# Hybrid decoder step on one core: all page loads of a round in one run, state loads in program order, the prompt tokens' attention norm on its own, one product on GpSimd

## The chip, the cores and the metric

The kernel runs on one core of a Trainium2 chip. The metric is the time of one execution on the device in microseconds (us). Work is issued by five queues: PE (TensorE: matmuls and, shown apart as PEld, their weight loads), DVE (VectorE), ACT (ScalarE), POOL (GpSimd) and SP (SyncE, which here issues nearly all DMA transfers). Each engine runs its own instructions in a fixed order; semaphores tie them together.

## The reference

One layer of a hybrid decoder for 256 prompt tokens and 8 samples of 8 new tokens each, 320 tokens (`NT`) in all, of width 2048. Everything is in float32.

```python
h = rmsnorm(x);  q, k, v, z, xbc, dt, glu = split(h @ w_in)
att = rmsnorm_per_head(stick_breaking_attention(q, k_all, v_all))
      # samples: 1024 past positions each, in pages of 128 from a pool, plus their own tokens
y   = rmsnorm(ssd(silu(conv(xbc)), dt, state) * silu(z))
u   = silu(layernorm(conv31(glu_u * sigmoid(glu_gate))))
x   = x + concat(att, y, u) @ w_out
x   = x + (silu(conv3(gate)) * val) @ w_down      # gate, val = split(rmsnorm(x) @ w_up)
return rmsnorm(x), new keys and values, all new states
```

Stick-breaking attention gives past position j the weight sigmoid(z_j) times the product of (1 - sigmoid(z_m)) over all m between j and the query. So it is computed from the newest page back to the oldest, with a running product as carry. The page table says which page of the pool holds which positions, so the address of a page load is known only at run time.

## The kernel before

**Weights.** Activations lie with channels on partitions and the 320 tokens in the free dimension. Every product with a weight matrix is built from *granules* of 128 x 1024 weights (512 KB). `wgran` loads one into a buffer `raw` (3 of them), ScalarE rounds it into `hi` (3), VectorE subtracts for the rest `lo` (3). `part` then does three matmuls for each of the eight 128x128 pieces: `hi` with the high and the low part of the activations and `lo` with the high part, 24 matmuls of 320 columns. A *block* is one 128-channel output of a projection: two granules of w_in, 48 matmuls into one `mm` tile. `win(b)` is block b of w_in. The sequence is: q, k, v and glu blocks, then `win(12)` to `win(23)` for xBC (each followed by a convolution in `g_xbc`, tiles `pre`, `xac`, `sgx`, `xs`), then z, then w_out, w_up and w_down. What the text calls block 20 is `win(20)`, in the instructions `mm_3829`; block 21 is `win(21)`, `mm_4070` before and `mm_4098` after.

**Work between the matmuls.** `part` calls `tick` after every fourth piece (12 matmuls). `tick` advances each generator of a list by one step (to its next `yield`), and so the small work is woven between the matmuls. A scheduler then orders the instructions of each engine. Inside `tc.high_priority()` an instruction is placed as early as its priority and its operands allow; weight loads and splits are written that way.

**The sample sweep.** `g_att` starts two `worker` generators. Each handles two pairs of samples, four *units* for each pair, from the newest quarter of the pages to the oldest; a unit is two samples times two pages. For a unit, `pages` reads four page numbers into registers of SP (from the second unit on through a copy `pu`, made on VectorE behind the previous unit's `m`), and `load` issues four DMAs of 256 KB into a `kt` or a `vt` tile. There are two buffers (`KVB`) for each of the tags `kt` and `vt`, shared by the two workers. So one *round* of both workers has 16 pages. A unit's steps: score matmuls (`mx<-kt,qpad`, 16), two sigmoids on ScalarE (`m` and `w`), a scan on VectorE (`cum`), the product of `w` and `cum` (line 566), two transposes (line 573), a copy to SBUF (line 577), 32 value matmuls (`av<-vt,m`), then the next unit's scores. When both workers have finished a group of samples, `g_pofin` transposes the result into `att`. The prompt's attention (`g_prompts`) ends earlier and writes `att[:, c, 64:]`.

**The attention norm.** `g_attnorm` starts when the whole sweep is done: squares on ScalarE, four matmuls with `blk2` that sum over a head's channels, a reciprocal root by Newton steps on VectorE (`rsq`, line 184, 12 instructions on the given number of columns), four matmuls with `blkT` that spread it over the channels, and a product with `att`.

**Behind w_out.** w_out is done in three passes over its 16 output blocks; the third (`mixY[1]`, granules of 128x512) also adds into `x2` and prepares `h2h`/`h2l`, the activations for w_up. `fst` is the FFN convolution's state, one load of 128x688. `g_state` runs in the w_up phase and updates 16 tiles `h0` of the SSD state.

Of the kernel before, what the change touches and what calls it, by code (L numbers as in the profile page):

```python
# [9 lines left out]
F32 = mybir.dt.float32  # L10
# [33 lines left out]
def body(ctx, tc, a):  # L44
# [469 lines left out]
    def pages(pr, hf, after=None):  # L514
        pu = pt[0:1].rearrange("p (s g) -> p s g", s=8)[:, 2 * pr:2 * pr + 2, 2 * hf:2 * hf + 2]
        if after is not None:
            q = ap.tile([1, 2, 2], I32, tag="pu", name=nm("pu"), bufs=2)
            V.scalar_tensor_tensor(out=q, in0=after[0:1, 0:4].bitcast(I32).rearrange("p (s g) -> p s g", s=2), scalar=0, in1=pu,
                                   op0=ALU.bitwise_and, op1=ALU.bitwise_or)
            pu = q  # L520
        with tc.high_priority():
            return [D.value_load(pu[0:1, e, j:j + 1], min_val=0, max_val=POOL - 1) for e in range(2) for j in range(2)]

    def load(tag, src, regs):
        t = ap.tile([P, 4, 512], F32, tag=tag, name=nm(tag), bufs=KVB)
        with tc.high_priority():
            for j, r in enumerate(regs):
                D.dma_start(out=t[:, j], in_=src[bass.ds(r, 1)].rearrange("a p n -> (a p) n"))
        return t


    def worker(prs):
        units = [(pr, hf) for pr in prs for hf in (3, 2, 1, 0)]
        regs = pages(*units[0])
        kt = load("kt", a["ck"], regs)
        vt = load("vt", a["cv"], regs)
        def scores(pr, kt):
            z = pmix()[:, 0:256]
            for e in range(2):
                for c in range(4):  # L540
                    mm(z[32 * c:32 * c + 32, :], qpad[:, c, 2 * pr + e], kt[:, 2 * e:2 * e + 2, c * P:(c + 1) * P], start=(e == 0), stop=(e == 1))
            return z

        yield
        z = scores(units[0][0], kt)
        for n, (pr, hf) in enumerate(units):
            gr = pr // 2
            if gr not in pos:
                pos[gr] = pav()
            po = [pos[gr][:, (2 * (pr % 2) + e) * P:(2 * (pr % 2) + e + 1) * P] for e in range(2)]  # L550
            yield
            m = keep(z, 256, nrow)
            w = take(z, 256, arow)
            if n + 1 < len(units):
                regs = pages(*units[n + 1], m)
                kt = load("kt", a["ck"], regs)
            for _ in range(2):
                yield
            while "self" not in done:
                yield  # L560
            if hf == 3:
                carry = cpair[:, pr:pr + 1]
            cum = ap.tile([P, 386], F32, tag="cum", name=nm("cum"), bufs=2)
            later(cum[:, 0:256], m, 256, carry)
            V.tensor_copy(cum[:, 256:257], carry)
            tt(V, w, w, cum[:, 1:257], ALU.mult)
            carry = car[:, pr:pr + 1]
            V.tensor_copy(carry, cum[:, 0:1])
            for _ in range(3):
                yield  # L570
            tp = pmix()[:, 0:256]
            for j in range(2):
                T.transpose(tp[:, j * P:(j + 1) * P], w[:, j * P:(j + 1) * P], ident)
            for _ in range(3):
                yield
            wT = t384("m")[:, 0:256]
            S.copy(wT, tp)
            for _ in range(2):
                yield
            if hf == 3:  # L580
                while len(gv) < 4 or any(g in gens for g in gv) or g_s[0] in gens:
                    yield
                for e in range(2):
                    for c in range(4):
                        mm(po[e][32 * c:32 * c + 32, :], wTm[:, 2 * pr + e, 32 * c:32 * c + 32], vtok[:, 0, c * P:(c + 1) * P],
                           start=(e == 0 and pr % 2 == 0))
            for e in range(2):
                for j in range(2):
                    for c in range(4):
                        mm(po[e][32 * c:32 * c + 32, :], wT[:, j * P + 32 * c:j * P + 32 * c + 32], vt[:, 2 * e + j, c * P:(c + 1) * P],  # L590
                           stop=(hf == 0 and j == 1))
            if n + 1 < len(units):
                z = scores(units[n + 1][0], kt)
                vt = load("vt", a["cv"], regs)
            if hf == 0:
                nseq[gr] += 1
                if nseq[gr] == 2:
                    gf.append(spawn(g_pofin(gr)))
# [72 lines left out]
        done.append("prompts")  # L671

    def g_attnorm():
        while gcv in gens:
            yield
        asq = rot.tile([P, 40, 38], F32, tag="uh", name="asq", bufs=1).rearrange("p a b -> p (a b)")[:, 0:4 * NT].rearrange("p (c t) -> p c t", c=4)
        act(asq, att, AF.Square)
        for _ in range(2):
            yield
        ps = pmix()  # L680
        for c in range(4):
            mm(ps[32 * c:32 * c + 32, :NT], blk2, asq[:, c], start=True, stop=True)
        ra = rsq(ps[:, 0:NT], NT, 64, "a", t320)
        for _ in range(3):
            yield
        for c in range(4):
            pb = pmix()
            mm(pb[:, :NT], blkT[:, c * P:(c + 1) * P], ra, start=True, stop=True)
            yield
            stt(V, att[:, c], att[:, c], col("gatt", c), pb[:, :NT], ALU.mult, ALU.mult)  # L690

    def g_att():
        g_s.append(spawn(g_self()))
        gp = spawn(g_prompts())
        wk = [spawn(worker([0, 2]))]
        for _ in range(5):
            yield
        wk.append(spawn(worker([1, 3])))
        while gp in gens or any(w in gens for w in wk) or any(g in gens for g in gf):
            yield  # L700
        done.append("att")
        yield from g_attnorm()
# [499 lines left out]
    h2h = [fp.tile([P, 8, NT], F32R, name=f"h2h{i}") for i in range(2)]  # L1202
    h2l = [t10("h2la", F32R), t10("h2lb", F32R)]
    acc2 = t320("acc2")
    for oc in range(KC):
        g0 = wgran(a["w_out"][oc, 1][:, 512:1024], 4)
        ps = pmain()
        mains(ps, [(g0, mixY[1][:, 0:4], mixY[1][:, 4:8])])
        xo = c2(x2, oc)
        with tc.high_priority():  # L1210
            tt(V, xo, xo, ps, ALU.add)
            act(c2(h2h, oc), xo, AF.Copy, scale=col("gffn", oc))
            stt(V, c2(h2l, oc), xo, col("gffn", oc), f32(c2(h2h, oc)), ALU.mult, ALU.subtract)
        sq = t320("sq")
        act(sq, xo, AF.Square)
        if oc == 0:
            G.tensor_copy(acc2, sq)
        else:
            tt(V if oc == KC - 1 else G, acc2, sq, acc2, ALU.add)
    rbs = []  # L1220


    fst = fp.tile([P, FC, 8, 2], F32, name="fst")
    D.dma_start(out=fst, in_=a["fst"])
    fso = fp.tile([P, FC, 18], F32, name="fso")
    gpre = [fp.tile([P, 338], F32, name=f"gpre{i}") for i in range(3)]
    for pr in gpre:
# [49 lines left out]
    def g_state():  # L1277
        for g in range(2):
            for k in range(2):
                ss = [2 * k, 4 + 2 * k, 2 * k + 1, 5 + 2 * k]  # L1280
                bm = fp.tile([P, P], F32, tag="bm", name=nm("bm"), bufs=2)
                hs = []
                for i, s in enumerate(ss):
                    r = slice(32 * i, 32 * i + 32)
                    ts(G, bm[r], bS[r, g], smask2[r, s:s + 1], ALU.mult)
                    h0 = fp.tile([P, 512], F32, tag="h0", name=nm("h0"), bufs=6)
                    D.dma_start(out=h0, in_=a["h0"][g, s])
                    tt(G, h0.rearrange("p (h d) -> p h d", h=8), h0.rearrange("p (h d) -> p h d", h=8),
                       ets[:, 16 * s + 8 * g:16 * s + 8 * g + 8].unsqueeze(2).to_broadcast([P, 8, 64]), ALU.mult)
                    hs.append(h0)  # L1290
                    for _ in range(3):
                        yield
                pss = [pmix() for _ in ss]
                for i in range(4):
                    r = slice(32 * i, 32 * i + 32)
                    mm(pss[i], bm[r], xS[g][r], start=True, stop=True)
                yield
                for i, s in enumerate(ss):
                    tt(V, hs[i], hs[i], pss[i], ALU.add)
                    D.dma_start(out=a["o_ss"][g, s], in_=hs[i])  # L1300
                    for _ in range(2):
                        yield
# [148 lines left out]
```

## Time and profile before

| what | value |
|---|---|
| time, median of 3 runs | 1464.94 us (1461.44 to 1466.72) |
| the profiled execution's own time | 1461.63 us |
| its span in the profile | 1459.8 us |
| TensorE busy | 1429.8 us, 98% of the span |
| VectorE busy | 902.6 us, 62% |
| ScalarE busy | 619.4 us, 42% |
| GpSimd busy | 192.4 us, 13% |
| data moved by DMA | 254.51 MB, 174 GB/s over the span |

The span runs from the first to the last instruction of the profiled execution; its own time is that span and what lies around it. Busy shares are means over stages: the sweep over the pages is one of them, and lies between about 80 and 280 us. What bounds a stage is read from the waits of the engine that is busiest there.

### The profile page before, as it was taken

To read this page: it belongs to the slowest core of one execution; us is meant where nothing else is said; L and a number is where in the kernel's file an instruction comes from. 1 tells how busy PE (TensorE), PEld (TensorE's weight loads), DVE (VectorE), ACT (ScalarE), POOL (GpSimd) and SP (SyncE) were. 2 spreads that over 40 slices of the span, in tenths; PEclk is the share of its full clock that TensorE was granted. 3 is DMA by queue.
4 is the path that set the end of the run, shared out by engine and by line. 5 is a ranking of instruction groups with operands and counts; after the bars stand their busy time and mean duration, and the time that the engine had idled before them with its cause. 6 is when DMAs were issued, how large, how long until landed. Compare 5 with 4: busy or idle time off the path is not lost.

```text
span 1459.8 us, 26793 instructions
## 1 busy us (share of the span) xinstructions
PE 1429.8 (98%) x10432; PEld 1386.5 (95%) x10432; DVE 902.6 (62%) x1636; ACT 619.4 (42%) x957; POOL 192.4 (13%) x321
## 2 busy tenths in 40 slices
PE   9999999899999999999999999999999999999996
PEld 8999998898889999999999999999999999999996
DVE  5577999868657885656545555455554555555455
ACT  6253555445544463334333443334433443433253
POOL 5000001112430431131100100001000110100000
PEclk9999999999999999999999999999999999999998
DMA  7566778774553554665544444544444444445442
GB/s 272 191 202 213 245 247 285 252 237 143 183 168 105 183 182 128 221 192 188 174 154 150 145 157 147 148 156 145 151 153 146 154 149 147 154 148 162 153 146 100
DMA packets 90880, 254.51 MB, mean 174 GB/s; under 512 B 10754, under 2 KB 17154, under 8 KB 90754
## 3 DMA queue, kind: packets, MB, share of 16 engines
q1 hardware_dynamic: 90754, 252.80, 54.6%
q8 instruction: 82, 1.34, 0.4%
q14 instruction: 44, 0.36, 0.1%
HBM read 242.67 MB, written 9.77 MB: 173 GB/s over the span
## 4 chain that ended last, share of the span: by engine, by line
PE 86%; DVE 8%; issue 2%; DMA 2%; ACT 1%; SPq 0%; DVEq 0%; ACTq 0%
PE mm L69 79%; PE mx L69 4%; DVE cfc L78 2%; DVE lo L72 2%; PE av L69 2%; DVE xac L78 1%; DMA kt<-in_ck 1%; DVE cum L479 0%; ACT hi L87 0%; DMA x0a<-in_x 0%; DMA raw<-in_w_out 0%; DVE w L72 0%; DVE x2a L72 0%; PE mx L962 0%; ACT uh L781 0%
## 5 line engine op out<-in xcount | busy, mean ns | idle before, releaser
L87 ACT ACTIVATE hi<-raw 128x1024 fp32r<-128x1024 f32 (+2 forms) x396 | 396.8, 1002 | 650.4 <-PE mm L69 401.2
L72 DVE TENSOR_TENSOR lo<-raw,hi 128x1024 fp32r<-128x1024 f32 (+2 forms) x396 | 467.3, 1180 | 266.7 <-ACT hi L87 265.6
L69 PE MATMUL mm<-h2h,hi 128*128 128x320 f32 x1376 | 425.9, 309 | 0.1
L69 PE MATMUL mm<-h2h,lo 128*128 128x320 f32 x1376 | 423.3, 308 | 0.0
L69 PEld LDWEIGHTS mm<-h2h,hi 128*128 128x128 f32 x1376 | 258.3, 188 | 3.4 <-issue 1.9
L69 PEld LDWEIGHTS mm<-h2h,lo 128*128 128x128 f32 x1376 | 258.3, 188 | 0.8 <-DVE lo L72 0.8
L69 PE MATMUL mm<-abh,hi 128*128 128x320 f32 x688 | 212.9, 309 | 0.4 <-DVE x2a L72 0.2
L69 PE MATMUL mm<-abh,lo 128*128 128x320 f32 x688 | 212.6, 309 | 0.0
L69 PE MATMUL mm<-h2la,hi 128*128 128x320 f32 x688 | 212.6, 309 | 0.0
L69 PE MATMUL mm<-h2lb,hi 128*128 128x320 f32 x688 | 212.6, 309 | 0.0
L69 PE MATMUL mm<-abl,hi 128*128 128x320 f32 x688 | 212.5, 309 | 0.0
L69 PEld LDWEIGHTS mm<-abh,hi 128*128 128x128 f32 x688 | 129.1, 188 | 1.2 <-issue 1.1
L69 PEld LDWEIGHTS mm<-abl,hi 128*128 128x128 f32 x688 | 129.2, 188 | 0.0
L69 PEld LDWEIGHTS mm<-h2lb,hi 128*128 128x128 f32 x688 | 129.1, 188 | 0.0
L69 PEld LDWEIGHTS mm<-abh,lo 128*128 128x128 f32 x688 | 129.1, 188 | 0.0
L69 PEld LDWEIGHTS mm<-h2la,hi 128*128 128x128 f32 x688 | 129.1, 188 | 0.0
L69 PE MATMUL mm<-xhb,hi 128*128 128x320 f32 x288 | 92.3, 321 | 0.0
L69 PE MATMUL mm<-xha,hi 128*128 128x320 f32 x288 | 90.9, 316 | 0.0
L69 PE MATMUL mm<-xla,hi 128*128 128x320 f32 x288 | 89.6, 311 | 1.3 <-DVE xla L78 1.3
L69 PE MATMUL mm<-xlb,hi 128*128 128x320 f32 x288 | 90.0, 312 | 0.0
L69 PE MATMUL mm<-xhb,lo 128*128 128x320 f32 x288 | 89.8, 312 | 0.0
L69 PE MATMUL mm<-xha,lo 128*128 128x320 f32 x288 | 89.1, 309 | 0.0
(355 smaller groups left out, 1932.1 us busy)
## 6 DMA issues: line engine op xcount, KB each, us to landing
raw<-in_w_up SPq DMA_DIRECT2D x172, 512.0 KB, 3.6
raw<-in_w_in SPq DMA_DIRECT2D x80, 512.0 KB, 3.7
raw<-in_w_dn SPq DMA_DIRECT2D x80, 512.0 KB, 3.5
kt<-in_ck SPq DMA_DIRECT2D x64, 256.0 KB, 3.9
vt<-in_cv SPq DMA_DIRECT2D x64, 256.0 KB, 4.6
h<-in_h SPq DMA_DIRECT2D x32, 256.0 KB, 4.3
raw<-in_w_out SPq DMA_DIRECT2D x16, 512.0 KB, 3.7
raw<-in_w_out SPq DMA_DIRECT2D x32, 256.0 KB, 2.7
```

The source lines that it names most:

```text
L69: T.matmul(out, lhsT, rhs, start=start, stop=stop, skip_group_check=True)
L72: e.tensor_tensor(out=out, in0=x, in1=y, op=op)
L78: e.scalar_tensor_tensor(out=out, in0=x, scalar=s, in1=y, op0=op0, op1=op1)
L87: S.activation(out, x, f, bias=bias, scale=scale)
```

## The change

1. `pages` and `load` put their work at a priority far above all other (`offset=10 ** 7`), so also above the weights.
2. The product of `w` and `cum` in the sample sweep (line 566) goes from VectorE (`V`) to GpSimd (`G`).
3. `g_attnorm` now handles the 64 sample columns only. A new generator `g_attnorm_p` handles the 256 prompt columns: it starts 24 ticks after the prompt's attention is done, during the sample sweep, and the sweep's end waits for it.
4. `fst` is loaded in the third pass of w_out, at output block 6, and `fst` and the `h0` loads of `g_state` are kept in program order (`keep_in_program_order`) rather than placed early by the scheduler.

```diff
--- before.py
+++ after.py
@@ -518,12 +518,12 @@
             V.scalar_tensor_tensor(out=q, in0=after[0:1, 0:4].bitcast(I32).rearrange("p (s g) -> p s g", s=2), scalar=0, in1=pu,
                                    op0=ALU.bitwise_and, op1=ALU.bitwise_or)
             pu = q
-        with tc.high_priority():
+        with tc.high_priority(offset=10 ** 7):
             return [D.value_load(pu[0:1, e, j:j + 1], min_val=0, max_val=POOL - 1) for e in range(2) for j in range(2)]
 
     def load(tag, src, regs):
         t = ap.tile([P, 4, 512], F32, tag=tag, name=nm(tag), bufs=KVB)
-        with tc.high_priority():
+        with tc.high_priority(offset=10 ** 7):
             for j, r in enumerate(regs):
                 D.dma_start(out=t[:, j], in_=src[bass.ds(r, 1)].rearrange("a p n -> (a p) n"))
         return t
@@ -563,7 +563,7 @@
             cum = ap.tile([P, 386], F32, tag="cum", name=nm("cum"), bufs=2)
             later(cum[:, 0:256], m, 256, carry)
             V.tensor_copy(cum[:, 256:257], carry)
-            tt(V, w, w, cum[:, 1:257], ALU.mult)
+            tt(G, w, w, cum[:, 1:257], ALU.mult)
             carry = car[:, pr:pr + 1]
             V.tensor_copy(carry, cum[:, 0:1])
             for _ in range(3):
@@ -671,32 +671,60 @@
         done.append("prompts")
 
     def g_attnorm():
-        while gcv in gens:
-            yield
-        asq = rot.tile([P, 40, 38], F32, tag="uh", name="asq", bufs=1).rearrange("p a b -> p (a b)")[:, 0:4 * NT].rearrange("p (c t) -> p c t", c=4)
-        act(asq, att, AF.Square)
+        b = slice(0, NS)
+        asq = t320("asq")[:, 0:256].rearrange("p (c t) -> p c t", c=4)
+        act(asq, att[:, :, b], AF.Square)
         for _ in range(2):
             yield
         ps = pmix()
         for c in range(4):
-            mm(ps[32 * c:32 * c + 32, :NT], blk2, asq[:, c], start=True, stop=True)
-        ra = rsq(ps[:, 0:NT], NT, 64, "a", t320)
+            mm(ps[32 * c:32 * c + 32, :NS], blk2, asq[:, c], start=True, stop=True)
+        ra = rsq(ps[:, 0:NS], NS, 64, "a")
+        for _ in range(2):
+            yield
+        pb = pmix()
+        for c in range(4):
+            mm(pb[:, NS * c:NS * c + NS], blkT[:, c * P:(c + 1) * P], ra, start=(c == 0), stop=True)
+        yield
+        for c in range(4):
+            stt(V, att[:, c, b], att[:, c, b], col("gatt", c), pb[:, NS * c:NS * c + NS], ALU.mult, ALU.mult)
+
+
+    def g_attnorm_p():
+        while "prompts" not in done:
+            yield
+        for _ in range(24):
+            yield
+        b = slice(NS, NT)
+        sq = [t384("m")[:, 0:256] for _ in range(4)]
+        for c in range(4):
+            act(sq[c], att[:, c, b], AF.Square)
         for _ in range(3):
+            yield
+        ps = pmix()
+        for c in range(4):
+            mm(ps[32 * c:32 * c + 32, :256], blk2, sq[c], start=True, stop=True)
+        ra = rsq(ps[:, 0:256], 256, 64, "a", lambda s: t320(s)[:, 0:256])
+        for _ in range(6):
             yield
         for c in range(4):
             pb = pmix()
-            mm(pb[:, :NT], blkT[:, c * P:(c + 1) * P], ra, start=True, stop=True)
-            yield
-            stt(V, att[:, c], att[:, c], col("gatt", c), pb[:, :NT], ALU.mult, ALU.mult)
+            mm(pb[:, :256], blkT[:, c * P:(c + 1) * P], ra, start=True, stop=True)
+            yield
+            stt(V, att[:, c, b], att[:, c, b], col("gatt", c), pb[:, :256], ALU.mult, ALU.mult)
+        done.append("attp")
 
     def g_att():
         g_s.append(spawn(g_self()))
         gp = spawn(g_prompts())
+        spawn(g_attnorm_p())
         wk = [spawn(worker([0, 2]))]
         for _ in range(5):
             yield
         wk.append(spawn(worker([1, 3])))
         while gp in gens or any(w in gens for w in wk) or any(g in gens for g in gf):
+            yield
+        while "attp" not in done:
             yield
         done.append("att")
         yield from g_attnorm()
@@ -1202,7 +1230,10 @@
     h2h = [fp.tile([P, 8, NT], F32R, name=f"h2h{i}") for i in range(2)]
     h2l = [t10("h2la", F32R), t10("h2lb", F32R)]
     acc2 = t320("acc2")
+    fst = fp.tile([P, FC, 8, 2], F32, name="fst")
     for oc in range(KC):
+        if oc == 6:
+            tc.keep_in_program_order(D.dma_start(out=fst, in_=a["fst"]))
         g0 = wgran(a["w_out"][oc, 1][:, 512:1024], 4)
         ps = pmain()
         mains(ps, [(g0, mixY[1][:, 0:4], mixY[1][:, 4:8])])
@@ -1220,8 +1251,6 @@
     rbs = []
 
 
-    fst = fp.tile([P, FC, 8, 2], F32, name="fst")
-    D.dma_start(out=fst, in_=a["fst"])
     fso = fp.tile([P, FC, 18], F32, name="fso")
     gpre = [fp.tile([P, 338], F32, name=f"gpre{i}") for i in range(3)]
     for pr in gpre:
@@ -1284,7 +1313,7 @@
                     r = slice(32 * i, 32 * i + 32)
                     ts(G, bm[r], bS[r, g], smask2[r, s:s + 1], ALU.mult)
                     h0 = fp.tile([P, 512], F32, tag="h0", name=nm("h0"), bufs=6)
-                    D.dma_start(out=h0, in_=a["h0"][g, s])
+                    tc.keep_in_program_order(D.dma_start(out=h0, in_=a["h0"][g, s]))
                     tt(G, h0.rearrange("p (h d) -> p h d", h=8), h0.rearrange("p (h d) -> p h d", h=8),
                        ets[:, 16 * s + 8 * g:16 * s + 8 * g + 8].unsqueeze(2).to_broadcast([P, 8, 64]), ALU.mult)
                     hs.append(h0)
```

`t384("m")`, `t320` and `pmix` are the existing rotating tiles of the attention part; `stt`, `tt` and `act` are the kernel's short names for operations of VectorE or GpSimd and of ScalarE, as the lines above show.

The orders below are lists of instructions as they stand in one engine's program. First SP (DMA issues) around the w_in granule `raw_2568`, the second one of `win(12)`. `TENSOR_LOAD pu` is the reading of a page number, `ISA` a register instruction. Before:

```order
L528 DMA kt_2299<-in_ck 128x512
L124 DMA raw_2568<-in_w_in 128x1024
L522 ISA x2
L522 TENSOR_LOAD pu_2308
L522 ISA x2
L522 TENSOR_LOAD pu_2261
L528 ISA
L528 DMA kt_2299<-in_ck 128x512
L124 DMA raw_2807<-in_w_in 128x1024
```

After, at the same granule:

```order
L528 ISA
L528 DMA kt_2346<-in_ck 128x512
L522 ISA x4
L124 DMA raw_2568<-in_w_in 128x1024
L124 DMA raw_2807<-in_w_in 128x1024
L124 DMA raw_2813<-in_w_in 128x1024
```

Pages and granules took turns before; now the last of 16 pages (`vt_2201`, `vt_2231`, `kt_2299`, `kt_2346`, four each) stands ahead of `raw_2568`, and granules follow each other.

Next TensorE inside block 20 (`mm_3829`), before. `vt_3493` and `vt_3531` are value pages of the last round but two, `kt_3608` and `kt_3655` key pages of the last round but one:

```order
L69 MATMUL mm_3829<-xhb,lo_3824 128x320
L69 MATMUL av_3066<-vt_3493,m_3842 32x128 x16
L69 MATMUL mx_3900<-kt_3608,qpad 32x256 x8
L69 MATMUL av_3066<-vt_3531,m_3844 32x128 x16
L69 MATMUL mx_3930<-kt_3655,qpad 32x256 x8
L69 MATMUL mm_3829<-xhb,hi_3825 128x320
```

After, behind the last matmul of the same block 20 (`mx_3967` are the sums of the prompt norm, `mx_4240` to `mx_4313` its products with `blkT`; `vt_3917`, `vt_3947` belong to the last round but one, the tiles from `kt_4029` on to the last):

```order
L69 MATMUL mm_3829<-xhb,lo_3824 128x320
L69 MATMUL mx_3967<-m_3842,blk_200 32x256
L69 MATMUL mx_3967<-m_3843,blk_200 32x256
L69 MATMUL mx_3967<-m_3844,blk_200 32x256
L69 MATMUL mx_3967<-m_3845,blk_200 32x256
L573 MATMUL mx_4210<-ident,w_3989 128x128 x2
L573 MATMUL mx_4213<-ident,w_4036 128x128 x2
L69 MATMUL av_3066<-vt_3917,m_4277 32x128 x16
L69 MATMUL av_3066<-vt_3947,m_4279 32x128 x16
L69 MATMUL mx_4240<-r_3973,blkT 128x256
```

And directly on, up to the first matmuls of block 21:

```order
L69 MATMUL mx_4313<-r_3973,blkT 128x256
L69 MATMUL mx_4356<-kt_4029,qpad 32x256 x8
L69 MATMUL mx_4386<-kt_4076,qpad 32x256 x8
L573 MATMUL mx_4534<-ident,w_4416 128x128 x2
L69 MATMUL av_3066<-vt_4365,m_4596 32x128
L573 MATMUL mx_4537<-ident,w_4420 128x128 x2
L69 MATMUL av_3066<-vt_4365,m_4596 32x128 x15
L69 MATMUL av_3066<-vt_4395,m_4598 32x128 x16
L609 MATMUL mx_4688<-ident,m_4689 128x128 x2
L609 MATMUL mx_4688<-ident,m_4706 128x128 x2
L69 MATMUL mm_4098<-xha,hi_4088 128x320
L69 MATMUL mm_4098<-xla,hi_4088 128x320
```

Before, each step of the sweep stood between matmuls of w_in, and the last rounds were spread over the matmuls of six more blocks (to the 69th granule of w_in). Now the last two rounds stand in one piece behind block 20 (the 57th and 58th granule), without a w_in matmul between them.

Last SP near the end of w_out, before:

```order
L1224 DMA fst<-in_fst 128x688
L124 DMA raw_6563<-in_w_out 128x512
L1287 DMA h_7283<-in_h 128x512
L124 DMA raw_6588<-in_w_out 128x512
L1287 DMA h_7323<-in_h 128x512
L1287 DMA h_7389<-in_h 128x512
L124 DMA raw_6613<-in_w_out 128x512
```

After:

```order
L124 DMA raw_6701<-in_w_out 128x512
L1236 DMA fst<-in_fst 128x688
L124 DMA raw_6727<-in_w_out 128x512
L124 DMA raw_6752<-in_w_out 128x512
L124 DMA raw_6777<-in_w_out 128x512
```

`fst` stands five granules of w_out later, and the `h0` tiles (`h` here) no longer stand between them.

## Rows read from the trace of the kernel before

**Rows 1.** Page: the span; busy time, share and instructions of each engine.

```profile
span 1459.8 us, 26793 instructions
PE 1429.8 (98%) x10432; PEld 1386.5 (95%) x10432; DVE 902.6 (62%) x1636; ACT 619.4 (42%) x957; POOL 192.4 (13%) x321
```

**Rows 2.** Waits of PE: waiting instruction, awaited one: us in total, times, longest.

```profile
PE mx L69 <- DMA kt<-in_ck: 7.0, 4, 2.3
PE mx L69 <- DVE r L78: 5.4, 3, 2.4
PE mm L69 <- DVE x2a L72: 2.4, 3, 1.5
PE mx L573 <- DVE w L72: 1.8, 1, 1.8
```

**Rows 3.** Timeline of PE: start, duration, instruction, [idle before <-releaser].

```profile
271.57 1.08 PE L69 MATMUL av<-vt,m 128*32 128x128 f32 x32
272.47 1.05 PE L69 MATMUL mx<-kt,qpad 128*32 128x256 f32 x16
...
278.77 0.81 PE L69 MATMUL mx<-kt,qpad 128*32 128x256 f32 x8 [1.98 <-DMA kt<-in_ck]
...
356.65 1.31 PE L69 MATMUL mx<-r,blkT 128*128 128x320 f32 x4 [1.16 <-DVE r L78]
```

**Rows 4.** Windows: busy of PE, PEld, DVE, ACT, POOL; clock, DMA share, GB/s.

```profile
144.00:148.00 4.00, 4.00 (x31) 3.64 (x30) 1.37 (x4) 2.17 (x4) 0.00 (x0) 1.00 1.04 388
200.00:250.00 50.00, 47.75 (x481) 45.27 (x483) 48.49 (x118) 27.94 (x61) 8.18 (x10) 1.00 0.84 274
279.20:282.60 3.40, 3.40 (x16) 3.09 (x13) 1.35 (x5) 0.84 (x2) 0.00 (x0) 0.51 1.02 357
```

**Rows 5.** Waits of the SP queue.

```profile
SPq L124 <- DVE lo L72: 975.5, 368, 5.8
```

**Rows 6.** Timeline of SP: DMA issues in the sweep.

```profile
139.48 5.11 SPq L528 DMA_DIRECT2D vt<-in_cv  x8
...
260.27 0.34 SPq L124 DMA_DIRECT2D raw<-in_w_in  x1
262.00 0.33 SPq L528 DMA_DIRECT2D kt<-in_ck  x1
```

**Rows 7.** Page, DMA issues: transfer, count, KB each, median us to landing.

```profile
raw<-in_w_in SPq DMA_DIRECT2D x80, 512.0 KB, 3.7
kt<-in_ck SPq DMA_DIRECT2D x64, 256.0 KB, 3.9
```

**Rows 8.** Chain in order of time: start, us, work.

```profile
118.42 7.04 PE mm L69 x48
```

**Rows 9.** Groups by shape, 60:345 (DVE 60:370): count | busy, mean ns | idle.

```profile
L87 ACT ACTIVATE hi<-raw 128x1024 fp32r<-128x1024 f32 x61 | 64.7, 1060 | 96.9 <-PE mm L69 57.4 <-issue 30.2 <-PE mx L69 3.1
L87 ACT ACTIVATE m<-mx,nrow 128x256 f32<-128x256 f32 x16 | 7.5, 470 | 15.6 <-PE mx L69 14.5 <-ACT w L87 0.9
...
L577 ACT COPY m<-mx 128x256 f32<-128x256 f32 x16 | 5.5, 370 | 2.0 <-PE mx L573 2.0
...
L72 DVE TENSOR_TENSOR lo<-raw,hi 128x1024 fp32r<-128x1024 f32 x65 | 80.9, 1244 | 25.0 <-ACT hi L87 24.8
...
L479 DVE TENSOR_TENSOR_SCAN cum<-m,car,zero 128x256 f32<-128x256 f32 x12 | 9.2, 763 | 2.8 <-ACT m L87 2.8
...
L72 DVE TENSOR_TENSOR q<-r 128x320 f32<-128x320 f32 x3 | 1.5, 485 | 0.0
```

**Rows 10.** Page, costliest groups, of GpSimd: count | busy, mean ns | idle.

```profile
L72 POOL TENSOR_TENSOR fac<-fac,rb 128x320 f32<-128x320 f32 x43 | 37.7, 876 | 41.8 <-ACT fac L87 41.8
```

**Rows 11.** Timeline of POOL and DVE at 273 to 277 us.

```profile
274.11 1.73 POOL L72 TENSOR_TENSOR xs<-xac,sgx 128x320 f32<-128x320 f32 x1 [0.71 <-ACT sgx L87]
...
273.45 0.55 DVE L78 SCALAR_TENSOR_TENSOR cfc<-uh,cols,cfc 128x320 f32<-128x320 f32 x1
...
275.05 1.14 DVE L78 SCALAR_TENSOR_TENSOR cfc<-uh,cols,cfc 128x320 f32<-128x320 f32 x1
```

## The prediction

> **What bounds the kernel now.** I read the page first [rows 1]: the profiled execution spans 1459.8 us (1461.63 us as timed, 1.8 us around it) and TensorE is busy in 98% of it. So there is little to win: whatever does not shorten a wait of TensorE or take matmul work away is hidden. Then the waits of TensorE [rows 2]: 7.0 us in four waits for key pages, 5.4 us in three waits for a reciprocal root (2.4 us of them at the kernel's end, which the change leaves alone), 2.4 us behind the add into `x2a`, 1.8 us before one transpose of `w`. Then the matmuls at those places [rows 3]: the score matmuls start after 1.98 us of idle time for `kt`, the normalising ones after 1.16 us for `r`. Last the windows [rows 4]: where two idle pieces stood close together, the granted clock falls to its lower level (1.2 GHz, 0.51 in the window) for 3.4 us, behind the key pages at 279 us and once more, in the same way, behind the attention norm at 361 us. At half rate 3.4 us do 1.7 us of work, so each costs 1.7 us more.
>
> Why the pages are late is on the SP queue. A weight load waits until its raw buffer is free, that is for a `lo` split [rows 5]; 368 of these waits add up to 975.5 us, and pages stand behind them in the same queue. In [rows 6] a weight load goes at 260.27 and the page behind it only at 262.00. The data path itself is not full over a whole sweep: DMA is busy 0.84 at 200 to 250 us, against 1.04 at 388 GB/s in a burst [rows 4].
>
> **The change, part by part.**
>
> *Pages in one run.* The two high priorities put all 16 pages of a round (8 of `vt`, 8 of `kt`, 256 KB each) ahead of the weights, as the first pair of orders shows. A round of 16 pages is 4.2 MB, 10.8 us at 388 GB/s; the issue alone runs at 5.1 us for 8 [rows 6], 10.2 us for 16. A page lands 3.9 us after its issue [rows 7]. A round of the sweep has about five weight granules of 3.5 us each (48 matmuls in 7.04 us [rows 8]) between one use and the next, so the pages land well before their score matmuls. I take all four waits as gone: -7.0 us, and with them the low clock behind them, -1.7 us.
>
> What stands behind the run are the weights, and TensorE waits for those. Three raw and three split buffers let SP issue a granule when TensorE has finished the sixth one before it and the split (1.06 + 1.24 us, [rows 9]) is done: 5 x 3.5 - 2.3 = 15.2 us ahead, plus the round's attention work on TensorE (two value products at 1.08, two scores at 1.05, [rows 3], some transposes at 0.15 each: 4.9 us) = 20.1 us. Needed: 10.8 us for the burst, 1.4 us for the 512 KB at the same rate, 2.3 us of landing beyond that (3.7 less 1.4, [rows 7]), 2.3 us of split = 16.8 us. It fits by 3.3 us, so I take 0; the bound above is a rival below.
>
> *One product on GpSimd.* The 256-column product has no row on GpSimd. Between a 128x320 product of 0.88 us [rows 10] and one of 1.73 us [rows 11] I take 1.2 us, as the latter is the nearer in place. In the sweep three ticks lie between product and transpose, so most of it is covered by matmuls. The one wait of 1.8 us came from the product standing behind a split and a convolution step on VectorE, and on GpSimd nothing stands ahead of it: -1.6 us (from 0 to -1.8).
>
> A multiply of GpSimd costs VectorE something too: beside the one at 274.11 a convolution step takes 1.14 us instead of 0.55 [rows 11]. The Trainium skill says more, in "SBUF — State Buffer" (the section on the shared port pair): a VectorE instruction with two SBUF inputs and a GpSimd instruction that reads SBUF take turns on an exclusive lock. By the row each of the 16 products costs VectorE 0.6 us and spares it 0.4 (the price of 256 columns below); by the rule it would cost up to the whole 1.2 us, 19 us in all against 6 spared, in a stretch where VectorE has 1.5 idle us in 50 [rows 4]. Either way VectorE pays first with convolution steps that nobody waits for, so the sum takes 0 and the rule becomes a rival.
>
> *Prompt norm in the sweep.* Work on TensorE is unchanged: the same four sums and four products, split into 256 and 64 columns. What is left at the old place is a chain over 64 columns instead of 320. The waits there are 5.4 - 2.4 = 3.0 us; VectorE's split loads still stand inside the chain and the next norm's chain follows, so I take half, -1.5 us (0 to -3.0), and the low clock at 361 us as avoided, -1.7 us.
>
> *The knot behind block 20.* This is the price, and it is seen only in the order. `vt_4365` and `vt_4395`, the last value pages, wait for buffers that the round before frees, and the weights of block 21 stand behind them in SP's queue. So TensorE's order has no weights there: behind block 20 come the norm's sums, the transposes and value products of the last round but one, the norm's four products, the scores of the last round, its transposes, its value products, the final transposes, and only then block 21. Before, six blocks' matmuls lay between these steps. Counted from the end of block 20:
> - The root's chain is 12 VectorE instructions of 256 columns; at 0.485 us for 320 columns [rows 9] that is about 0.39 each, 4.7 us, and six steps of the block's own convolution lie in between, at the same price 2.3 us: `r` at 7.6 us with the sums (four matmuls at the pace of 48 in 7.04 us, 0.6). The transposes and value products of the round before (2.8 us) hide in it. The last pages of `kt` wait for the same round's page numbers and land at about the same time.
> - Four normalising products: two of 320 columns took 1.31 us [rows 3], so 2.1 us. Two scores 2.1 us: 11.8.
> - Then a bare chain for the second worker [rows 9]: sigmoid 0.47, scan 0.76, product on GpSimd 1.2, transpose 0.3, copy 0.37, value product 1.1, two copies 0.74, the `hi` split behind them in ScalarE's order 1.06, the `lo` split 1.24, 7.2 us together, and 0.8 that I put for some ten handovers: 8.0 us, so block 21 runs from 19.8 us.
> Matmuls in it: 0.6 + 2.8 + 2.1 + 2.1 + 0.6 + 2.2 + 0.6 = 11.0 us, so TensorE idles 8.8 us. The idle pieces lie as closely as those before the two falls of the clock, so I add two low stretches, one inside and one under block 21: 2 x 1.7 = 3.4. Sum +12.2 us. Bounds: 6 (clock stays up, root at 5 us) and 18 (three low stretches, a slow product, pages 3 us late).
>
> *State loads held in place.* Before, `fst` and six `h0` loads were pulled between the last w_out granules, and the wait behind `x2a` (2.4 us) is there. Now `fst` comes alone before a later granule and the `h0` loads come in w_up, where raw buffers are far ahead. -2.2 us (0 to -2.4).
>
> Sum: -7.0 - 1.7 - 1.6 - 1.5 - 1.7 - 2.2 + 12.2 = -3.5, so 1458.1 us against the profiled execution's 1461.63. The median of the three runs is 3.3 us above that execution; I put the forecast on the median, 1464.94 - 3.5 = **1461.4 us**. A measurement of this kernel can tell about 0.3% (4.4 us) from no change, so this counts as the same.
>
> **The rivals.**
> 1. *A cheap knot.* The clock stays up and the root comes early: +6 in place of +12.2, with all else as above: 1464.94 - 9.7 = 1455.2. For it: the longest wait for `kt` [rows 2], in the same sweep at 226 us and alone, brought no fall. Against: the knot has four of them in a row.
> 2. *Weights starve behind the pages* (slower). If SP must wait inside the run, for a page number or a freed buffer, by more than the 3.3 us of room, TensorE waits for a weight in each of six rounds. With 5.0 us inside, 1.7 us over the room, that is six times 1.7 and one low stretch: +12, 1473. For it: DMA is at 1.04 in bursts and at 0.84 over the sweep. Against: the buffers and numbers are freed within one short group of matmuls.
> 3. *A long knot.* Late pages or a third low stretch: +18, so 1467.2. It counts as the same.
> 4. *The lock.* GpSimd's products stop VectorE long enough to delay splits at 200 to 250 us, where it is busy 48.49 of 50 us: 16 x 0.8 us (1.2 held up less 0.4 spared), half of it on splits that are waited for: +6.4, 1467.8. Against: the row's 0.6 us would leave 0.2 of the 0.8. The rule of the Trainium skill above ("SBUF — State Buffer") is the one by which it would happen.
>
> **How the numbers follow.** The sum has 0.45, the cheap knot 0.25, starving 0.15, the long knot 0.1, the lock 0.05. The sum's own range is 1456 to 1467 (knot 8 to 18). For the whole, 1454 to 1470 leaves out most of the starving case and the best of the cheap one. Faster by over 0.3%: the cheap knot and a sixth of the sum's case, 0.32. Slower: starving, and a part of the long knot and the lock, 0.2. The same: 0.48.
>
> **What would show it.** Right: no wait for `kt` in 80 to 265 us; TensorE 15 to 25 us without w_in matmuls at about 270 to 292 us, with the granted clock at half there; no wait for `x2a` near 500 us. Wrong: waits for `hi` or `lo` right behind the page runs (rival 2), a knot whose idle time is under 5 or over 14 us, or VectorE's splits late beside GpSimd's products.

## The result, and the profile after

The changed kernel takes 1474.34 us (median of 4 runs, 1473.91 to 1475.97) against 1463.19 us of the kernel before (4 runs). The ratio is 1.0076, with a 95% interval of 1.0051 to 1.0102: slower by 11 us, where the prediction had 1461.4 us and no measurable change, with 0.2 on slower. The page of the changed kernel, its span and busy times:

```profile
span 1473.0 us, 26854 instructions
PE 1441.0 (98%) x10448; PEld 1394.5 (95%) x10448; DVE 902.0 (61%) x1636; ACT 620.5 (42%) x961; POOL 208.9 (14%) x337
```

The span is 13.2 us longer than in [rows 1], and TensorE's busy time rose by 11.2 us although its work is almost the same: part of that work ran at the lower clock. Now the waits of TensorE in the changed kernel:

```profile
PE mx L69 <- DVE r L78: 7.3, 3, 3.6
PE mm L69 <- ACT hi L87: 3.9, 4, 1.8
PE mm L69 <- DVE lo L72: 3.4, 3, 1.8
PE mx L69 <- ACT m L654: 1.2, 1, 1.2
PE mx L573 <- POOL w L72: 1.2, 1, 1.2
```

Against [rows 2], the waits for `kt` and `x2a` are gone, as forecast. New are 7.3 us of waits for weights (`hi` and `lo`), a wait of 3.6 us for the prompt norm's root, and 1.2 us for the product, now on GpSimd. Where the clock fell, in windows of the changed kernel (columns as in [rows 4]):

```profile
217.00:228.00 11.00, 8.00 (x86) 6.23 (x88) 8.77 (x17) 7.06 (x14) 1.80 (x3) 0.69 0.39 102
247.00:256.00 9.00, 6.94 (x65) 5.89 (x54) 7.93 (x13) 3.31 (x4) 1.49 (x2) 0.81 0.47 134
...
287.00:317.00 30.00, 22.03 (x210) 16.74 (x209) 16.08 (x47) 8.79 (x18) 3.43 (x5) 0.72 0.78 261
292.30:299.00 6.70, 5.81 (x28) 3.52 (x32) 2.63 (x6) 0.59 (x2) 0.86 (x1) 0.50 0.95 287
302.60:305.80 3.20, 3.20 (x58) 2.65 (x60) 0.00 (x0) 0.37 (x1) 0.00 (x0) 0.50 0.49 201
309.40:316.00 6.60, 6.06 (x23) 6.06 (x24) 4.34 (x11) 0.49 (x1) 0.00 (x0) 0.50 0.98 332
```

A granted clock of 0.69 over 11 us is (1 - 0.69) x 11 / 0.5 = 6.8 us at the lower level (1.2 GHz); the second row gives 3.4 us, the third 16.8 us. The kernel before had two such stretches of 3.4 us outside its end.

Two places hold the loss. First, **the weights behind the page runs**. SP, ScalarE, VectorE and TensorE of the changed kernel around the granule that follows the run at 194 us:

```profile
194.12 4.96 SPq L528 DMA_DIRECT2D vt<-in_cv  x8
199.60 8.43 SPq L528 DMA_DIRECT2D kt<-in_ck  x8
208.68 15.71 SPq L124 DMA_DIRECT2D raw<-in_w_in  x5
...
214.51 0.20 ACT L903 COPY sso<-pre 128x3 f32<-128x3 f32 x1 [3.53 <-DVE pre L72]
...
217.47 0.47 ACT L87 ACTIVATE sgx<-xac 128x320 f32<-128x320 f32 x1 [1.54 <-DVE xac L78]
217.84 1.04 ACT L87 ACTIVATE hi<-raw 128x1024 fp32r<-128x1024 f32 x1
...
217.35 2.79 DVE L78 SCALAR_TENSOR_TENSOR cfc<-uh,cols,cfc 128x320 f32<-128x320 f32 x4
220.06 1.22 DVE L72 TENSOR_TENSOR lo<-raw,hi 128x1024 fp32r<-128x1024 f32 x1
...
218.94 0.41 PE L69 MATMUL mm<-xha,hi 128*128 128x320 f32 x1 [1.16 <-ACT hi L87]
...
221.33 0.63 PE L69 MATMUL mm<-xha,lo 128*128 128x320 f32 x1 [1.84 <-DVE lo L72]
```

The run takes from 194.12 to 208.03, 13.9 us, not the 10.2 us that the prediction took for 16 issues: `kt x8` alone takes 8.43 us. Between these issues SP reads eight page numbers, some 0.27 us each, with register instructions behind them; for a number or a buffer that was not ready it waited only 0.4 us in this run. Then the granule issued at 208.68 is split only at 217.84 and 220.06. Transfers in this stretch landed after a median of 4.6 us:

```profile
raw<-in_w_in SPq DMA_DIRECT2D x3, 512.0 KB, 4.6
```

The rest of the delay is the order on the other engines: `hi` stands behind `sgx`, which waits for a convolution on VectorE, and `lo` behind four convolution steps. By that median the granule had landed at 213.3 us, while ScalarE stood idle up to 214.51 for the step ahead in its order. In the kernel before, the next split stood ahead of that step (line 903 is line 875 there):

```profile
211.08 1.06 ACT L87 ACTIVATE hi<-raw 128x1024 fp32r<-128x1024 f32 x1 [1.31 <-issue]
...
214.47 0.19 ACT L875 COPY sso<-pre 128x3 f32<-128x3 f32 x1 [2.07 <-DVE pre L72]
```

From issue to the end of `lo` (221.28) are 12.6 us; the prediction reckoned 6.0. What SP waits for among the pages, over the whole span:

```profile
SPq L528 <- PE av L69: 20.2, 7, 8.4
...
SPq L522 <- DVE pu L518: 15.5, 5, 7.6
```

The first are value buffers that the round's value products free, the second page numbers; in the kernel before they were 4.6 and 5.5 us. Most of them lie elsewhere than the run shown above: 13.0 of the 20.2 us at 241 to 262 us, in a later round, and 11.9 of the 15.5 us at 80 to 120 us, where TensorE waited for no weight.

Second, **the knot behind block 20** (the "bare stretch" of the expectations below), TensorE without the matmuls of blocks. It lies at 286 to 308 us, where the prediction put it at about 270 to 292:

```profile
286.09 0.64 PE L69 MATMUL mx<-m,blk 128*32 128x256 f32 x8
286.66 0.66 PE L573 MATMUL mx<-ident,w 128*128 128x128 f32 x4
287.62 1.96 PE L69 MATMUL av<-vt,m 128*32 128x128 f32 x64 [0.30 <-ACT m L577]
293.19 3.75 PE L69 MATMUL mx<-r,blkT 128*128 128x256 f32 x8 [3.62 <-DVE r L78]
296.88 2.97 PE L69 MATMUL mx<-kt,qpad 128*32 128x256 f32 x32
301.00 0.44 PE L573 MATMUL mx<-ident,w 128*128 128x128 f32 x2 [1.16 <-POOL w L72]
301.90 0.41 PE L69 MATMUL av<-vt,m 128*32 128x128 f32 x2 [0.46 <-ACT m L577]
302.35 0.65 PE L573 MATMUL mx<-ident,w 128*128 128x128 f32 x2
302.94 3.35 PE L69 MATMUL av<-vt,m 128*32 128x128 f32 x62
306.82 0.71 PE L609 MATMUL mx<-ident,m 128*128 128x128 f32 x4 [0.54 <-ACT m L606]
...
308.05 0.41 PE L69 MATMUL mm<-xha,hi 128*128 128x320 f32 x1 [0.52 <-ACT hi L87]
...
309.94 0.63 PE L69 MATMUL mm<-xha,lo 128*128 128x320 f32 x1 [1.32 <-DVE lo L72]
```

It is the order that was read, step for step, and the times in brackets add up to 7.9 us idle. At the lower clock the four normalising products take 3.75 us (1.31 for two of 320 columns in [rows 3]), the scores 2.97.

### The profile page after: what moved, and what is told of

It is laid out like the page before. It is cut to its first block, busy times and chain, and to the rows that moved or that the text cites. A ratio compares the mean times of both kernels' runs of the same rounds, so it can differ in the third digit from the quotient of the medians.

```text
span 1473.0 us, 26854 instructions
## 1 busy us (share of the span) xinstructions
PE 1441.0 (98%) x10448; PEld 1394.5 (95%) x10448; DVE 902.0 (61%) x1636; ACT 620.5 (42%) x961; POOL 208.9 (14%) x337
## 4 chain that ended last, share of the span: by engine, by line
PE 90%; DVE 6%; issue 1%; ACT 1%; SPq 1%; DMA 1%; POOL 0%; DVEq 0%; POOLq 0%; ACTq 0%
PE mm L69 82%; PE mx L69 5%; PE av L69 2%; DVE cfc L78 2%; DVE lo L72 1%; DVE xac L78 1%; SPq L528 1%; DVE cum L479 0%; DMA x0a<-in_x 0%; DVE x2b L72 0%; SPq L522 0%; ACT hi L87 0%; DMA kt<-in_ck 0%; PE mx L990 0%; DVE x2a L72 0%
```

## The experiments

Ratios are to the kernel before on the same chip. The theory: the page run causes the loss, half by starved weights, half by the knot; the other parts gain.

**1. No page run.** In `pages` and `load`, the other parts stay:

```diff
-        with tc.high_priority(offset=10 ** 7):
+        with tc.high_priority():
```

> The changed kernel with the page loads and page numbers back at the ordinary high priority; the other three parts stay. Theory (the run of pages causes the whole loss, by starved weights in the sweep, by the bare stretch behind block 20 and by the low clock behind both): the losses of the sweep go and the gains of the other parts stay, some 7 us at the attention norm, 4 us at the end of w_out, 2 us at the product: 1450 us (1447 to 1454), with the waits for key pages of the kernel before back, 5 to 8 us. Rival (GpSimd's products or the prompt norm in the sweep delay the splits): 1460 or more, with waits for hi or lo at 215 to 250 us.

Measured: 1456.04 us, ratio 0.9941 (0.9926 to 0.9957), against 1.0076 with the run. So the run costs (1.0076 - 0.9941) x 1464.5 = 20 us, and without it the other parts make the kernel faster by 8 us. The theory stands; the number was 2 us over the window. The forecast had counted 7 us for the norm and 2 for the product, where experiments 7 and 8 below find some 4 us and nothing. The waits for pages are not the reason; they came back as forecast, 6.3 us in all against 7.0 before:

```profile
PE mx L69 <- DMA kt<-in_ck: 6.3, 3, 3.5
```

**2. The page run alone**, on the kernel before (the edit above, reversed).

> The kernel before with the page run alone (page loads and page numbers at the far higher priority). Theory: all of the loss and none of the gains of the other parts: starved weights cost some 13 us and the bare stretch some 12 (without the prompt norm's root in it): 1480 us (1475 to 1486). Rival (the loss needs the prompt norm's root or the GpSimd product in the bare stretch): under 1470.

Measured: 1474.62 us, ratio 1.0075 (1.0056 to 1.0093). All of the loss, but 5 us less than forecast and just under its range: the run alone is as slow as the whole change, and 2.7 us of waits for `kt` are left in it. Experiment 10 says where the other parts' gain goes: with the run in place, norm and state loads still give (1.0075 - 1.0036) x 1464.5 = 6 us, and the product takes them back.

**3. The last two rounds' value pages at the old priority**, so that the weights of block 21 do not stand behind them:

```diff
-    def load(tag, src, regs):
+    def load(tag, src, regs, off=10 ** 7):
-        with tc.high_priority(offset=10 ** 7):
+        with tc.high_priority(offset=off):
-                vt = load("vt", a["cv"], regs)
+                vt = load("vt", a["cv"], regs, 10 ** 7 if n + 1 < 6 else None)
```

> The changed kernel with the value pages of the last two units of each worker at the ordinary priority, so that the weights of block 21 no longer stand behind them; the pages of the earlier rounds stay in one run. Theory (starved weights and the bare stretch each cost some 13 us): the bare stretch goes, the waits for hi and lo at 215 to 280 us stay: 1460 us (1457 to 1464). Rival A (the bare stretch is nearly the whole loss): 1450. Rival B (starving is the whole loss, the bare stretch only shifts work): 1471 or more.

Measured: 1459.41 us, ratio 0.9962 (0.9947 to 0.9977). As the theory had it. The knot is worth 0.0114 x 1464.5 = 17 us, and the starved weights stay:

```profile
PE mm L69 <- ACT hi L87: 3.3, 3, 1.8
PE mm L69 <- DVE lo L72: 2.1, 2, 1.8
```

**4. Only the keys run**: in `load`, `offset=10 ** 7 if tag == "kt" else None`.

> The changed kernel with the far higher priority for page numbers and key pages only; value pages go at the ordinary priority between the weights. Theory (SP stands inside the run waiting for value buffers that a round's value products free, and the weights starve behind it; key buffers are free long before): the waits for hi and lo go, the bare stretch goes, the waits for key pages stay away: 1446 us (1443 to 1451). Rival (any run of eight or more pages starves the weights, whatever it waits for): waits for hi or lo of over 4 us stay, 1455 or more.

Measured: 1456.93 us, ratio 0.9946 (0.993 to 0.9962): 11 us over the forecast, 6 over its range, and no better than no run at all. The time is the rival's; the waits that the rival named are not there. The waits for `kt` are gone, and those for `hi` and `lo` are down to 1.7 us, but one of 2.58 us has taken their place:

```profile
278.06 1.06 ACT L87 ACTIVATE hi<-raw 128x1024 fp32r<-128x1024 f32 x1 [1.00 <-DMA raw<-in_w_in]
279.02 0.35 ACT L577 COPY m<-mx 128x256 f32<-128x256 f32 x1
...
279.42 0.84 PE L69 MATMUL av<-vt,m 128*32 128x128 f32 x21 [2.58 <-ACT m L577]
```

The raw weights, issued behind the eight keys at 272.03 us, land 6 us later; `hi` waits for them at the head of ScalarE's order, and the copy that the value product needs waits behind `hi`. A late weight so stops attention work too.

**5. Pages on another queue.** The page numbers are read and the pages issued by GpSimd:

```diff
-            return [D.value_load(pu[0:1, e, j:j + 1], ...
+            return [G.value_load(pu[0:1, e, j:j + 1], ...
-                D.dma_start(out=t[:, j], in_=src...
+                G.dma_start(out=t[:, j], in_=src...
```

> The changed kernel with the page numbers read and the page loads issued by GpSimd's queue in place of SP's; priorities, product and all else stay. Theory (the weights starve because they stand in one queue behind page loads that wait for a freed value buffer or a page number; the transfers themselves have room): no wait for hi or lo at 215 to 280 us, no bare stretch, no waits for kt: 1452 us (1448 to 1456), if an issue on that queue costs little. Rival (the burst of 16 pages fills the data path and the weights land late whichever queue issues them): waits for hi or lo of 4 us and more stay, 1460 or more. Third way: GpSimd's own products stand behind the waiting page loads, and the transposes wait for them: waits of mx at line 573 of 5 us and more.

Measured: 1460.82 us, ratio 0.9978 (0.9967 to 0.999), 9 us over the forecast. The waits for weights are nearly gone, with the same transfers in runs of up to 16, so the data path was not what starved them. The third way came true beside it:

```profile
PE mx L573 <- POOL w L72: 6.6, 9, 1.8
...
PE mm L69 <- DVE lo L72: 0.5, 1, 0.5
```

GpSimd's own order shows why; the two products come behind the last page:

```profile
241.09 0.54 POOL L528 DMA_DIRECT2D kt<-in_ck  x1 [0.75 <-issue]
241.66 2.39 POOL L72 TENSOR_TENSOR w<-w,cum 128x256 f32<-128x256 f32 x2
```

The Trainium skill says in "Trainium Kernel Development and Optimization" (Key Constraints) that the queues of SP, ScalarE and GpSimd use the same DMA engines, and that issuing from several saves only issue time. Here it saved more: a second queue also takes what one stream waits for and reads out of the other's way.

**6. The same, with the product back on VectorE** (`tt(V, w, w, cum[:, 1:257], ALU.mult)`).

> As the run before it (pages on GpSimd's queue), with the product of w and cum back on VectorE, so that no product stands behind a waiting page load. If products behind page loads are what costs: 3 us and more under the run before it. If not: within 2 us of it, a little above it by the product's own wait (2 us).

Measured: 1454.15 us, ratio 0.9935 (0.9915 to 0.9955), 6.7 us under the run before it. The 6.6 us of waits for the product on GpSimd are gone, with 1.8 us for the product on VectorE in their place, so products behind page loads are what the profile shows to cost there. The time alone does not show it: experiment 10 finds 6 us for the same move with the pages on SP's queue.

**7. Norm and state loads alone** (no page run, product on VectorE).

> The changed kernel without the page run and with the product back on VectorE: norm and state loads alone. Theory (the product on GpSimd takes away one wait of 1.8 us and costs little): 2 us above the first experiment's 1456.0, 1458 (1456 to 1460). Rival (GpSimd's products hold VectorE up and so cost more than they save): at or under 1455.

Measured: 1454.76 us, ratio 0.9931 (0.9915 to 0.9948), where 1458 was forecast and the rival had 1455 or less. Against the first experiment's 0.9941 the product on GpSimd is worth nothing that can be told; the intervals overlap widely.

**8. The prompt tokens' norm alone**, on the kernel before.

> The kernel before with the prompt tokens' norm in the sweep alone. Theory (3 to 4 us of waits and of low clock at the old place go, and the sums and products at the new place lie behind matmuls): 4 us under the kernel before, 1460 to 1461, and 4 us above the run before it in this call, which has the state loads too. Rival (the chain only moves, with its waits): within 1.5 us of the kernel before.

Measured: 1459.75 us, ratio 0.998 (0.9968 to 0.9992): 3.6 us under the kernel before by the medians, as forecast, and 5.0 us above experiment 7 (7 us by the ratios), so that is what the state loads give. In the window from 480 to 600 us, first of the norm alone and then with the state loads:

```profile
480.00:600.00 120.00, 116.91 (x790) 114.17 (x789) 88.84 (x159) 60.02 (x104) 44.73 (x59) 1.00 0.54 171
```

```profile
480.00:600.00 120.00, 120.00 (x823) 118.97 (x822) 88.89 (x166) 61.98 (x107) 36.98 (x53) 1.00 0.53 164
```

3.1 us of idle time of TensorE are gone there; where the rest of the 5 us lies stays open.

**9. Half of the knot**: as experiment 3, with `n + 1 < 7`, so only the last round's value pages are spread.

> The changed kernel with only the value pages of each worker's last unit at the ordinary priority. By the order, the first half of the bare stretch stays (the prompt norm's sums, the root, its products, the last scores) and the weights of block 21 then come ahead of the last transposes and value products. Theory (the bare stretch costs by its chain of handovers and by the low clock behind each piece, some 15 us in all): the idle piece of 3.6 us ahead of the norm's products and one or two low stretches stay, the second half (4 us idle, 10 us of low clock) goes: 1466 us (1463 to 1469), between the changed kernel and the third experiment's 1459.4. Rival (the root's wait in the first half is the whole price): 1472 or more. Other rival (only the last chain costs): 1460.

Measured: 1465.67 us, ratio 1.0011 (0.9999 to 1.0022), as the theory had it: of the 17 us, the first half with the root costs 0.0049 x 1464.5 = 7 us, the second half 10. One detail went against it. Here, too, TensorE idles 3.62 us before the norm's products:

```profile
291.32 1.96 PE L69 MATMUL mx<-r,blkT 128*128 128x256 f32 x8 [3.62 <-DVE r L78]
```

but the products take 1.96 us and not 3.75: in this execution the clock did not fall there, though it fell in the changed kernel's after an idle piece of the same length. It was the fastest of the ten executions and had the highest mean clock (0.994, the others 0.991 to 0.993), so the profile is not typical of them.

**10. The whole change, with the product back on VectorE.**

> The changed kernel with the product of w and cum back on VectorE, page run and all else as changed. Theory (the product is worth nothing either way, as without the run): within 2 us of the changed kernel, 1473 to 1476. Rival (on GpSimd it lengthens the bare chain, where nothing covers it): 1471 or less. Rival of the prediction (on VectorE it stands behind splits and costs a wait of 2 us): 1476 or more.

Measured: 1469.62 us, ratio 1.0036 (1.0021 to 1.005): 0.0040 x 1464.5 = 6 us under the changed kernel. The theory (within 2 us) failed: with the run in place the product on GpSimd does cost, though how much is rough, since the two intervals nearly touch. The time is the first rival's, but its longer chain is not seen: the wait before the last transposes is 1.06 us where it was 1.16, and the knot's idle time is 7.9 us in both. The clock differs:

```profile
287.00:317.00 30.00, 22.44 (x210) 18.02 (x199) 17.92 (x50) 9.55 (x18) 2.15 (x3) 0.83 0.79 265
```

(1 - 0.83) x 30 / 0.5 = 10.2 us at the lower level against 16.8 us, worth 3.3 us; the spans of the two profiled executions differ by 3.4 us. Why the clock falls less often with the product on VectorE was not settled.

## Why the prediction was wrong

**Key pages, -8.7: the waits went, the gain is not shown.** No wait for `kt` is left. But experiments 4 and 6 are without these waits too, and are no faster than experiments 1 and 7, which have 6.3 and 5.8 us of them: there other waits took their place, among them one for a copy on ScalarE (2.6 and 2.7 us).

**"It fits by 3.3 us, so I take 0": this step failed.** Measured are 7.3 us of waits for weights, of which 0.52 + 1.32 lie behind the knot, so 5.5 in three rounds of the sweep, and low stretches of 6.8 and 3.4 us behind them. TensorE was busy in these for 6.0 and 3.3 us, half of which is lost, 4.6: 10.1 us in all. What the step left out is the order of ScalarE and VectorE. The room was reckoned from issue, transfer and split alone, and by these the granule issued at 208.68 would have been in time: landed at 213.3, split by 215.6, while TensorE had work up to 217.8. The splits that stand behind convolution steps made up most of the 6.6 us by which the path was longer. The run was also 3 us longer than reckoned, with the reading of eight page numbers inside it.

Rival 2 had named the outcome and given 1473 us, with a chance of 0.15; that the number comes so near is partly luck. It had priced six rounds at 1.7 us; three paid, 3.0, 2.1 and 0.4 us. Its condition, waits of over 3.3 us inside the run, was not met in the costliest round, with 0.4 us of waiting inside the run. Its "against" was wrong all the same: value buffers are not always freed quickly, as the 13.0 us at 241 to 262 us show, in a wait of up to 8.4. That the split slipped in ScalarE's order because its load stands later in the queue is read from the two traces, and was not tested by itself.

**The knot, +12.2: right in place, too small.** The idle time was 8.8 in the prediction and 7.9 us in the profile. The clock was mis-sized: I took two stretches of 3.4 us, and there were 17 us. In them TensorE was busy 5.81 + 3.20 + 6.06 = 15.1 us, of which half is lost, 7.5 us where I had 3.4. Together 15.4 us; experiment 3 says 17. My longest knot, rival 3 with +18, had a chance of 0.1.

**The product, -1.6: failed.** The wait of 1.8 us did go (one of 1.2 us came in the knot), but the product gave nothing without the run (experiment 7) and cost some 6 us with it (experiment 10). In the two profiles the difference is 3.4 us and nearly all clock; its cause stays open. It was not the lock as rival 4 priced it: VectorE's `lo` splits took 1239 ns on the mean, 1244 before, the product took less than the 1.2 us that I reckoned,

```profile
L72 POOL TENSOR_TENSOR w<-w,cum 128x256 f32<-128x256 f32 x16 | 13.0, 813 | 189.9 <-DVE cum L565 151.8 <-ACT xac L87 8.6 <-DVE cfc L78 8.6
```

and only one scan of the sweep ran beside one. It took 1.06 us instead of 0.75:

```profile
299.39 0.75 DVE L479 TENSOR_TENSOR_SCAN cum<-m,car,zero 128x256 f32<-128x256 f32 x1 [1.92 <-ACT m L87]
...
300.43 1.06 DVE L479 TENSOR_TENSOR_SCAN cum<-m,car,zero 128x256 f32<-128x256 f32 x1
...
300.31 0.64 POOL L72 TENSOR_TENSOR w<-w,cum 128x256 f32<-128x256 f32 x1 [6.28 <-DVE cum L565]
```

That agrees in direction with the rule of the Trainium skill that the prediction weighed ("SBUF — State Buffer", the shared port pair), at a quarter of the price that it was given there. Over the sweep the convolution steps paid a little: the 120 of `cfc` took 583 ns on the mean where they had taken 568, and the 36 wide ones of `xac` 502 where they had taken 477, 2.7 us in all. Against that, VectorE's own products of 256 columns fell from 10.4 to 3.2 us.

**The norm, -3.2: held in size** (-3.6, experiment 8), in part by luck. The waits for the root fell by 1.5 us, as reckoned. The low stretch near the old place is gone in the profile of experiment 8, but one of 3.4 us is there again in those of experiments 1 and 3 to 7, with the norm in the sweep; from experiment 7:

```profile
354.60:358.20 3.60, 3.60 (x16) 3.60 (x15) 3.17 (x14) 2.88 (x4) 0.94 (x1) 0.53 0.13 53
```

**The state loads, -2.2: too small** (-5.0, experiments 7 and 8).

With what was measured the sum comes out, roughly: -8.7 for the keys (not shown by itself), +10.1 for starved weights, +15.4 to 17 for the knot, -3.6, -5.0, and 1 to 6 for the product, about +9 to +16 against the measured +11. In steps that were each measured: norm and state loads alone are at 0.9931 (experiment 7), with the run at 1.0036 (10), with the product as well at 1.0076, so -10, +15 and +6 us. The run costs 11 us alone (2), 15 us beside the norm and the state loads, 20 us with the product too (1). Norm and state loads give 8.5 us by the medians, and the product gives nothing by itself. Experiments 1, 4, 6 and 7 (0.9931 to 0.9946) cannot be told from each other; experiment 7 keeps one queue and leaves the product where it was.

## What to carry to other kernels

When loads share a queue with the stream that feeds the busiest engine, moving a run of them ahead of it holds the stream up by all the time that the run takes there, with its issues, address reads and waits; ask what each load in the run waits for, and whether that itself stands behind the stream. When you reckon whether a late transfer fits, count all the way to the engine that uses it, with the work that stands ahead of its follow-up steps in the other engines' orders. A gap in the dense stream can cost more than its idle time: in this knot 7.9 us of idle time brought 7.5 us of low clock, while in the profile of experiment 9 an idle piece of 3.62 us brought none.

## What the runs showed of the hardware

The clock's falls are not the same in two executions of one kernel with one order. The 18 executions of the kernel before beside experiment 10 have mean granted clocks of 0.990 to 0.994 and spans of 1459.2 to 1465.3 us, the longest at the lowest clock; those of experiment 10 go from 0.989 (1471.4 us) to 0.993 (1464.2 us). So a good part of the spread between the runs of this kernel, some 0.4%, goes with the clock. In the changed kernel falls lasted up to 6.8 us, as in the window from 217 to 228 us, and in experiment 2 one lasted 17 us (290.5 to 307.5 us, clock 0.51), where both falls of the kernel before, ahead of its end, lasted 3.4 us.
